# New tables of instruction order for five engines in a hybrid decoder layer on one core

## The chip, the core and the metric

The kernel runs as one program on one core of a Trainium2 chip. The core has five engines with instruction streams of their own: TensorE (PE in the rows; its weight loads are listed apart as PEld), VectorE (DVE), ScalarE (ACT), GpSimd (POOL) and SyncE (SP, which issues the transfers). An engine takes its instructions strictly in the order in which they stand in its stream, and an instruction waits there until what it depends on in other streams is done. The metric is the time of one execution on the device, in microseconds (us); less is better.

## What is computed

One layer of a decoder for a prompt of 512 tokens and 8 sample sequences of one token each, with a width of 1024. The two share all weights, so each matmul runs over 512 + 8 columns, in two halves of 256 and 264. Cut to what matters here:

```python
h = x @ w_in                                       # one input projection for both head groups
# sparse attention: scores with slopes, softmax; compressed, selected and window branch, gated
o_nsa = gates[..., 0:1] * o_cmp + gates[..., 1:2] * o_slc + gates[..., 2:3] * o_win
# gated DeltaNet: convolution, silu, l2norm, then chunks of 64 tokens
qkv, new_gbuf = causal_dwconv(h[..., C_GQKV:C_GA], gdn_buf, gdn_conv_w)
gc = jnp.cumsum(g, axis=-1)
A = jnp.einsum('nbhid,nbhjd->nbhij', kb, k) * dec_strict + jnp.eye(C, dtype=jnp.float32)
X = lax.linalg.triangular_solve(A, rhs, left_side=True, lower=True)
...
vn = val_c - jnp.einsum('bhcd,bhde->bhce', kcd_c, S)
S = S * jnp.exp(gl)[..., None, None] + jnp.einsum('bhcd,bhce->bhde', kend_c, vn)
...
x = layer_norm(DN_ALPHA * x + mix @ w_out, ln_g[0], ln_b[0])
up = x @ ffn_w_up
hg, new_fbuf = causal_dwconv(up[..., :D_FF], ffn_buf, ffn_conv_w)
ffn = (jax.nn.gelu(hg, approximate=False) * up[..., D_FF:]) @ ffn_w_down
x = layer_norm(DN_ALPHA * x + ffn, ln_g[1], ln_b[1])
ple = jax.nn.sigmoid(x @ ple_w_gate) * (p.astype(x.dtype) @ ple_w_proj)
x = layer_norm(DN_ALPHA * x + ple, ln_g[2], ln_b[2])
```

## The kernel before

**Matmuls.** Every weight tile comes from memory as float32 (`raw`, two buffers). ScalarE rounds it to a short form `wh` (L249), and VectorE, or GpSimd for some tiles, subtracts to get the remainder `wl` (L250). `product` then sums three products into a PSUM bank `mm`: `wh` with the high part of the activations (L411), `wl` with the high part (L412), `wh` with the low part (L415). A tile of the input projection with 8 blocks of 128 rows so takes 24 matmuls for each half. Activations carry the same split: `xh`, `xl` for the input, `x1h`, `x1l` behind a norm, `mh`, `ml` for the mixed heads.

**Stages in the profile.** From 0 to about 250 us run the input projection and, woven into it, the convolution of the DeltaNet (L519, L520), its l2norm (L541, L549), the gates and cumulative sums (`g` L588, `gc` L591 and L595), the decay matrices (`exps` L623, `E` L627), `kk` (L634) with the masked products `Lc` and `Lb` (L640, L643), the triangular solve by recursion (`X`, L653 to L682), and the scan over chunks (`vn` L805, `Sd` L810, `S` L814, `Sst` L816, `o` L838, normed at L842 and L845 and transposed to `oT` at L848). The decode step of the samples' DeltaNet state runs beside it: products `stmp` (L862 to L868), the reduction L869, and `so` (L874), a small matmul that needs a PSUM bank of the tag `pg`, of which there are two; VectorE's `inn` (L790) reads `qk` from such a bank. To about 410 us follow attention and output projection: the split keys `KHL` (cast on GpSimd L972, remainder on VectorE L974) and queries `Qs` (L987), scores `S` (L1001), maxima and scaling (`mn` L1008, `rs` L1012 and L1013, `P` L1018 on GpSimd), the copies `qbd` (L1125), the compressed branch `cs` (L1087 to L1099). Then the norm (`acc` L1264, mean `mu` L1274, `R` L1278, L1295 and L1300, splits L1297 to L1302), the FFN's up and down projections to about 780 us, and the layer embedding with the last norms.

**What sets the order.** The code is written in the order of several lists, but what counts is `in_order`. Behind the whole program it takes, for each engine, the instructions as written and chains them anew in the sequence that the table `RUNS` gives: a string of steps, in which `+24` means 24 places on, `-3` back, and `*7` a step repeated. So `RUNS` alone decides which instruction of an engine stands behind which; what is computed, on which engine, and in which buffers does not depend on it. Where several tiles share a tag, the same function also fixes the order of their first uses.

Of the kernel before, what the change touches and what calls it, by code (L numbers as in the profile page):

```python
# [36 lines left out]
def _constants():  # L37
# [70 lines left out]
    SP='+3 -4*3 +2 -2 +1 +3 +1 -6*2 +11 +40 +3 -57 +3 -3 +3 +51 -52 -3 +4 -3 +3 +41 -46 +6 -4 +3*3 +91*2 -93*3 -8 -2 +88 +1 -2 -82 +82*3 +1 -2 -86*2 +2 +2*3 -7 -2 +7 -6*2 +28 -9 +3 +1 -5 +6 +1 +9 -38 +7 +3*2 -5 +4 -5 +4 -5 -11*5 +1 -2 +32 +1 -16 +17 -17 +16 -8 +10 -2 -20*4 +1 -2 +1*2 +14 -12 +11 -11*2 +10 -2 +1 -6 -5*2 +9 +1 +2 +3 +12 -24 +85*2 -86 +1 +32 -33 +1 +43 +1 -43 -4*2 +12 +1*10 +21 -22*3 +20*2 -21*13 +9 -9 +1 +6 -6 +6 -5 +5*2 -5 +4*3 -6 +7*3 -5*2 +3*2 +1 +1*4 -7 +1 +4*2 +2*8 +3 -2 +1*6 -9 -2 +9*5 +2*4 -6*2 +4*15 +2*5 -7*2 +5*5 +2*3 -5*2 +3*13 +11*3 -12*3 -5*2 +3*6 +3 +2*3 -5*2 +3*17 +2*2 -4 +5 -6 +5*3 -6*2',  # L108
)

def in_order(tc, nc):

    of = dict(PE=mybir.EngineType.PE, ACT=mybir.EngineType.Activation, DVE=mybir.EngineType.DVE,
              POOL=mybir.EngineType.Pool, SP=mybir.EngineType.SP)
# [26 lines left out]
def body(tc, nc, ctx, I, O, dbg=None):  # L141
    V, S, G, PE = nc.vector, nc.scalar, nc.gpsimd, nc.tensor
    if dbg is None:
# [1544 lines left out]
```

## Time and profile before

| | us |
|---|---|
| median of 3 runs | 888.88 |
| the three runs | 888.88, 886.75, 889.32 |
| the profiled execution | 887.08 |
| its span in the trace | 885.1 |

The span is what the trace covers from the first to the last instruction; 2.0 us of the profiled execution lie outside it. The clock that was granted to TensorE is 0.995 of full speed over that execution. In the rows below, "busy" is the time in which an engine has an instruction running; several alike are drawn together as "x4" with one duration for all. Waits are put down to the event that ended them.

### The profile page before, as it was taken

Reading aid. Unit: us, or ns where it says so; the run is one execution under the profiler, and the core shown is the slowest. Engines: PE = TensorE matmul, PEld = TensorE weight load, DVE = VectorE, ACT = ScalarE, POOL = GpSimd, SP = SyncE. Lnnn points to the kernel's source line nnn. Section 1 sums busy time; section 2 is a strip of 40 time slices with the busy share of each in tenths; the row PEclk is TensorE's granted clock in tenths of the full one; section 3 lists DMA queues with packets and bytes.
Section 4 is the critical chain, followed back from the end, with each engine's and each line's share of the span. In section 5 each row is a group of like instructions: output and inputs, shape, how many; then the busy total and the mean of one; then the engine's idle time right before and its main releaser. Section 6 shows DMA issues by size and latency. Waiting matters only on the chain.

```text
span 885.1 us, 19223 instructions
## 1 busy us (share of the span) xinstructions
PE 850.9 (96%) x7661; PEld 793.1 (90%) x7661; DVE 585.3 (66%) x1312; ACT 426.8 (48%) x940; POOL 198.4 (22%) x303
## 2 busy tenths in 40 slices
PE   7999999998999999999999999999999999999996
PEld 5988998997888667978899999999999999999985
DVE  3578996678779877788854553344563255577977
ACT  4554538433357886665543432244442144435745
POOL 1133031454413533306710000000000000005332
PEclk9999999999999999999999999999999999999999
DMA  7321323323226240244423243233344133243302
GB/s 210 88 71 50 97 75 100 88 77 81 76 77 209 60 152 18 85 122 120 128 63 118 83 122 96 76 108 104 97 120 121 48 96 90 85 139 119 120 1 97
DMA packets 139112, 85.98 MB, mean 97 GB/s; under 512 B 8318, under 2 KB 130656, under 8 KB 138880
## 3 DMA queue, kind: packets, MB, share of 16 engines
q1 hardware_dynamic: 139024, 84.77, 33.0%
q8 instruction: 60, 0.98, 0.5%
q14 instruction: 28, 0.23, 0.1%
HBM read 79.54 MB, written 7.36 MB: 98 GB/s over the span
## 4 chain that ended last, share of the span: by engine, by line
PE 70%; DVE 16%; ACT 5%; DMA 4%; issue 3%; POOL 1%; SPq 1%; DVEq 0%; ACTq 0%
PE mm L411 18%; PE mm L415 18%; PE mm L412 18%; DVE wl L250 2%; DMA raw<-in_w_out_dram 2%; DVE R L1295 1%; PE PT L1037 1%; DVE qkv L519 1%; DVE X L655 1%; PE S L1001 1%; PE var L1286 1%; DMA raw<-in_w_in_dram 1%; PE pgate L1615 1%; PE pgate L1617 1%; DVE KHL L974 1%
## 5 line engine op out<-in xcount | busy, mean ns | idle before, releaser
L249 ACT CAST wh<-raw 128x512 fp32r<-128x512 f32 x198 | 119.5, 609 | 212.1 <-PE mm L415 189.5
L250 DVE TENSOR_TENSOR wl<-raw,wh 128x512 fp32r<-128x512 f32 (+1 forms) x190 | 131.5, 699 | 125.2 <-ACT wh L249 123.9
L411 PE MATMUL mm<-x1h,wh 128*128 128x256 f32 (+1 forms) x704 | 195.7, 285 | 0.6 <-ACT fcb L1419 0.6
L412 PE MATMUL mm<-x1h,wl 128*128 128x264 f32 (+1 forms) x704 | 195.7, 283 | 0.2 <-POOL wl L250 0.2
L415 PE MATMUL mm<-x1l,wh 128*128 128x264 f32 (+1 forms) x704 | 195.6, 283 | 0.0
L411 PEld LDWEIGHTS mm<-x1h,wh 128*128 128x128 f32 x704 | 131.1, 188 | 1.6 <-ACT fcb L1419 0.8
L412 PEld LDWEIGHTS mm<-x1h,wl 128*128 128x128 f32 x704 | 131.7, 188 | 0.5 <-POOL wl L250 0.4
L415 PEld LDWEIGHTS mm<-x1l,wh 128*128 128x128 f32 x704 | 131.5, 188 | 0.0
L411 PE MATMUL mm<-xh,wh 128*128 128x256 f32 (+1 forms) x408 | 118.7, 298 | 0.3 <-DVE mT L483 0.2
L412 PE MATMUL mm<-xh,wl 128*128 128x264 f32 (+1 forms) x408 | 115.2, 286 | 0.0
L415 PE MATMUL mm<-xl,wh 128*128 128x264 f32 (+1 forms) x408 | 114.3, 286 | 0.0
L412 PE MATMUL mm<-hhl,wl 128*128 128x256 f32 (+1 forms) x352 | 97.9, 283 | 0.0
L411 PE MATMUL mm<-hhl,wh 128*128 128x264 f32 (+1 forms) x352 | 97.0, 284 | 0.3 <-DVE R L1507 0.3
L415 PE MATMUL mm<-hhl,wh 128*128 128x256 f32 (+1 forms) x352 | 96.7, 283 | 0.0
L411 PEld LDWEIGHTS mm<-xh,wh 128*128 128x128 f32 x408 | 76.8, 190 | 4.5 <-ACT z L203 0.7
L1431 POOL COPY last<-fcb 128x10 f32<-128x10 f32 x22 | 8.9, 405 | 310.5 <-ACT fcb L1419 294.7
L412 PEld LDWEIGHTS mm<-xh,wl 128*128 128x128 f32 x408 | 77.1, 190 | 0.8 <-issue 0.5
L415 PEld LDWEIGHTS mm<-xl,wh 128*128 128x128 f32 x408 | 76.9, 190 | 0.4 <-issue 0.2
L412 PEld LDWEIGHTS mm<-hhl,wl 128*128 128x128 f32 x352 | 65.7, 188 | 0.1
L411 PEld LDWEIGHTS mm<-hhl,wh 128*128 128x128 f32 x352 | 65.3, 188 | 0.5 <-DVE R L1507 0.5
L415 PEld LDWEIGHTS mm<-hhl,wh 128*128 128x128 f32 x352 | 65.2, 188 | 0.1
L1300 POOL TENSOR_SCALAR R<-R,vec 128x264 f32<-128x264 f32 (+1 forms) x40 | 28.7, 730 | 67.9 <-ACT x1h L1297 50.3
(453 smaller groups left out, 1868.8 us busy)
## 6 DMA issues: line engine op xcount, KB each, us to landing
raw<-in_ffn_w_up_dram SPq DMA_DIRECT2D x44, 512.0 KB
raw<-in_w_in_dram SPq DMA_DIRECT2D x25, 512.0 KB
raw<-in_w_out_dram SPq DMA_DIRECT2D x32, 256.0 KB
raw<-in_ffn_w_down_dram SPq DMA_DIRECT2D x16, 512.0 KB
pg<-in_cache_nsa_kv_dram SPq DMA_DIRECT2D x16, 256.0 KB
praw<-in_ple_w_gate_dram SPq DMA_DIRECT2D x8, 512.0 KB
raw<-in_ffn_w_down_dram SPq DMA_DIRECT2D x8, 384.0 KB
xr<-in_x_prompt_dram SPq DMA_DIRECT2D x16, 128.0 KB
```

Of the source, the lines that this page charges most:

```text
L249: both = (S.copy(th[:, :k1 - k0, :M], raw[:, k0:k1, :M]), low.tensor_tensor(tl[:, :k1 - k0, :M], raw[:, k0:k1, :M], th[:, :k1 - k0, :M], o ...
L250: low.tensor_tensor(tl[:, :k1 - k0, :M], raw[:, k0:k1, :M], th[:, :k1 - k0, :M], op=ALU.subtract))
L411: PE.matmul(o, hs[k], rh[hv][k], start=(k == ks[0]), stop=False)
L412: PE.matmul(o, ls[k], rh[hv][k], start=False, stop=False)
L415: PE.matmul(o, hs[k], rl[hv][k], start=False, stop=(k == ks[-1]))
L519: V.scalar_tensor_tensor(y[:, :T], cb[:, k:k + T], gcw[:, k, j:j + 1], y[:, :T], op0=ALU.mult, op1=ALU.add)
L655: V.tensor_tensor(X[:, j + 1:32, 0:j + 1], X[:, j + 1:32, 0:j + 1], tv, op=ALU.add)
L974: V.tensor_tensor(kl[d2 * 64:d2 * 64 + 64, :T], kvf[f][r0, :T], kh[r0, :T], op=ALU.subtract)
L1001: PE.matmul(ps[:, :wm], q_[:, ts_], kh[:, :wm], start=True, stop=False)
L1037: PE.transpose(pt[:, g4 * 128:g4 * 128 + 128], P[g4][:, st * 128:st * 128 + 128], ident)
L1300: G.tensor_scalar(r, r, b_, 1.0, op0=ALU.add, op1=ALU.mult)
L1431: G.tensor_copy(rows[:, :, f % 4], cb[:, 512:522])
```

## The change

Only the five strings of `RUNS` differ, one for each engine. A line of it:

```diff
-    POOL='+63 -64 +61 +40 +14 -118 +1 -2 +1*2 +1 +1 -4 +1 +1*6 +18 -19 +2*2 +14*2 +1 -22 +51 -48 ...
+    POOL='+63 -64 +61 +40 +14 -118 +1 -2 +1*2 +1 +1 -4 +1 +1*6 +18*3 +1 -23 +2*2 -4 +4*2 -6 +18 ...
```

Every engine has exactly the instructions that it had, with the same operands: 6759 on TensorE, 1314 on VectorE, 867 on ScalarE, 308 on GpSimd, 359 on SyncE. 3372 of TensorE's stand at another place, 630 of VectorE's, 308 of ScalarE's and 105 of GpSimd's; most by a few places.

The first place is TensorE's stream behind the convolution's tile `mm_1135`, where `l2s` and `l` are the l2norm's sums and `gc` the first cumulative sums; `mm_1184` and `mm_1210` are the next tile of the input projection. Rows with a minus stood there before, rows with a plus stand there now:

```order
 L412 MATMUL mm_1135<-xh_15_86,wl_1106 128x264
 L415 MATMUL mm_1135<-xl_16_87,wh_1105 128x264
-L541 MATMUL l2s_640<-sq_632,cst 128x8
-L541 MATMUL l2s_640<-sq_634,cst 128x8
+L541 MATMUL l2s_640<-sq_636,cst 128x8
 L549 MATMUL l_84_648<-sq_632,cst 128x512
-L549 MATMUL l_85_654<-sq_634,cst 128x512
-L591 MATMUL gc_613<-g,cst 128x32 x2
-L549 MATMUL l_86_660<-sq_636,cst 128x512
 L411 MATMUL mm_1184<-xh_1_72,wh_1176 128x256
 L411 MATMUL mm_1210<-xh_1_72,wh_1176 128x264
```

`gc` and two of the `l` leave this place. The first `gc` now stands 33 matmuls later, with `exps` behind it, and the second 73 matmuls later, behind the tile `mm_1258`.

The second place is TensorE's stream between the two halves `mm_2834` and `mm_2860` of one tile:

```order
 L412 MATMUL mm_2834<-xh_15_86,wl_2831 128x256
 L415 MATMUL mm_2834<-xl_16_87,wh_2830 128x256
-L874 MATMUL so_2922<-sgd_2004,cst 64x64 x3
 L411 MATMUL mm_2860<-xh_1_72,wh_2826 128x264
 L412 MATMUL mm_2860<-xh_1_72,wl_2827 128x264
```

The `so` that stood between the two halves is gone from there, and the 24 matmuls of `mm_2860` follow at once. At their end the stream reads:

```order
 L415 MATMUL mm_2860<-xl_16_87,wh_2830 128x264
-L848 MATMUL oT_3004<-cst,o_2958 128x128 x4
+L848 MATMUL oT_3004<-cst,o_2958 128x128
+L874 MATMUL so_2922<-sgd_2004,cst 64x64 x3
 L751 MATMUL ktm_3013<-cst,qkv_295 128x128
+L848 MATMUL oT_3004<-cst,o_2958 128x128
 L751 MATMUL ktm_3013<-cst,qkv_370 128x128
+L919 MATMUL kvT_2888<-cst,kvf_339_2823 128x128 x2
 L751 MATMUL ktm_3013<-cst,qkv_444 128x128
+L848 MATMUL oT_3004<-cst,o_2958 128x128 x2
```

Three of the four matmuls of `so` now stand behind `mm_2860` and behind one transpose `oT`, which needs `o` from VectorE.

The third place is VectorE's stream in the attention. `qbd` are copies of 64x8 elements that set up the samples' queries; `rs_3918` are the factors of four heads, on which GpSimd's scaling `P_3933` waits. Before:

```order
L1087 TENSOR_TENSOR cs_3843<-cs_3838,cb_3844 128x512
L1125 COPY qbd_3989<-qks 64x8 x5
L1008 ISA P_4199,mn_4183<-S_4196,dist_3278 128x256
L1008 ISA mn_4183 128x1
L1012 RECIPROCAL rs_3918<-rs_3918 128x4
L1125 COPY qbd_3989<-qks 64x8
L1008 ISA P_4188,mn_4183<-S_4191,dist_3278 128x256
L1008 ISA mn_4183 128x1
L1013 TENSOR_TENSOR rs_3918<-rs_3918,sig 128x4
L1090 TENSOR_REDUCE cmn_3847<-cs_3843 128x32
L1125 COPY qbd_3989<-qks 64x8 x2
L1008 ISA P_4199,mn_4183<-S_4202,dist_3278 128x256
```

And now:

```order
L1125 COPY qbd_3989<-qks 64x8 x6
L1012 RECIPROCAL rs_3918<-rs_3918 128x4
L1125 COPY qbd_3989<-qks 64x8 x2
L1013 TENSOR_TENSOR rs_3918<-rs_3918,sig 128x4
L1008 ISA P_4199,mn_4183<-S_4196,dist_3278 128x256
L1008 ISA mn_4183 128x1
L1087 TENSOR_TENSOR cs_3843<-cs_3838,cb_3844 128x512
L1008 ISA P_4188,mn_4183<-S_4191,dist_3278 128x256
L1008 ISA mn_4183 128x1
L1090 TENSOR_REDUCE cmn_3847<-cs_3843 128x32
```

All eight copies stand ahead of the finished `rs_3918` (L1013), and `cs` and its reduction behind it. On GpSimd, the stream changes at the norm at 430 us, too: the first scaling L1300 of `R_517` stands one place earlier, ahead of the `wl` with which it stood in turn, and a second one comes before the last of the four `wl`.

## Rows read from the trace of the kernel before

**Rows 1.** The page: span, busy time by engine, chain by engine, one group
```profile
span 885.1 us, 19223 instructions
...
PE 850.9 (96%) x7661; PEld 793.1 (90%) x7661; DVE 585.3 (66%) x1312; ACT 426.8 (48%) x940; POOL 198.4 (22%) x303
...
PE 70%; DVE 16%; ACT 5%; DMA 4%; issue 3%; POOL 1%; SPq 1%; DVEq 0%; ACTq 0%
...
L1300 POOL TENSOR_SCALAR R<-R,vec 128x264 f32<-128x264 f32 (+1 forms) x40 | 28.7, 730 | 67.9 <-ACT x1h L1297 50.3
```

**Rows 2.** Busy us (x instructions) of PE, PEld, DVE, ACT, POOL in two stages
```profile
100.00:150.00 50.00, 48.96 (x558) 45.31 (x558) 43.12 (x94) 30.35 (x58) 11.86 (x16) 1.00 0.32 85
...
450.00:500.00 50.00, 50.00 (x412) 49.44 (x411) 23.70 (x48) 18.40 (x35) 1.96 (x9) 1.00 0.31 96
```

**Rows 3.** Waits of TensorE by releaser: us in total, times, longest us
```profile
PE so L874 <- DVE inn L790: 2.7, 1, 2.7
PE S L1001 <- DVE mn L1008: 2.2, 3, 1.1
...
PE mu L1274 <- DVE acc L1264: 1.4, 1, 1.4
...
PE gc L591 <- DVE g L588: 1.1, 1, 1.1
...
PE X L682 <- ACT Ys L676: 0.8, 1, 0.8
...
PE soT L886 <- DVE inn L790: 0.7, 1, 0.7
```

**Rows 4.** Duration ns min/median/max of four lines' instructions on VectorE
```profile
L1295 DVE SCALAR_TENSOR_TENSOR R<-R,vec,rstd x40: 473/486/1521, 401.1 to 872.9; 128x264 f32<-128x264 f32 x24, 128x256 f32<-128x256 f32 x16
...
L1278 DVE TENSOR_TENSOR R<-R,mu x40: 410/422/429, 391.8 to 858.8; 128x264 f32<-128x264 f32 x24, 128x256 f32<-128x256 f32 x16
...
L250 DVE TENSOR_TENSOR wl<-raw,wh x190: 404/690/1756, 19.5 to 790.6; 128x512 fp32r<-128x512 f32 x182, 128x256 fp32r<-128x256 f32 x8
...
L987 DVE SCALAR_TENSOR_TENSOR Qs<-qf,Qs x8: 685/1006/1395, 222.7 to 267.8; 64x512 fp32r<-64x512 f32 x8
```

**Rows 5.** Timeline (start us, us), 200 to 206 us, VectorE, then GpSimd
```profile
200.18 2.35 DVE L250 TENSOR_TENSOR wl<-raw,wh 128x512 fp32r<-128x512 f32 x2
...
203.47 2.71 DVE L974 TENSOR_TENSOR KHL<-kvf,KHL 64x512 fp32r<-64x512 f32 x3
...
200.15 1.83 POOL L931 TENSOR_TENSOR VV<-kvo,VV 128x512 fp32r<-128x512 f32 x1
201.94 3.70 POOL L972 CAST KHL<-kvf 64x512 fp32r<-64x512 f32 x4
```

**Rows 6.** Timeline, 222 to 227 us, VectorE, then GpSimd
```profile
222.67 4.07 DVE L987 SCALAR_TENSOR_TENSOR Qs<-qf,Qs 64x512 fp32r<-64x512 f32 x4 [0.26 <-ACT Qs L986]
...
222.52 3.67 POOL L972 CAST KHL<-kvf 64x512 fp32r<-64x512 f32 x4
```

**Rows 7.** Timeline, 278 to 283 us, VectorE, then GpSimd
```profile
278.00 0.78 DVE L1125 COPY qbd<-qks 64x8 f32<-64x8 f32 x5
...
280.69 1.61 DVE L1125 COPY qbd<-qks 64x8 f32<-64x8 f32 x2
...
280.21 1.04 POOL L1018 TENSOR_TENSOR P<-P,rs 128x512 f32<-128x512 f32 x1 [8.18 <-DVE rs L1013]
```

**Rows 8.** Timeline, 418 to 434 us, VectorE and GpSimd in turn
```profile
419.28 2.64 DVE L1264 TENSOR_TENSOR acc<-acc,R 128x264 f32<-128x264 f32 x2
...
418.92 4.13 POOL L250 TENSOR_TENSOR wl<-raw,wh 128x512 fp32r<-128x512 f32 x3 [0.65 <-ACT wh L249]
...
430.47 3.17 DVE L1295 SCALAR_TENSOR_TENSOR R<-R,vec,rstd 128x264 f32<-128x264 f32 x3 [2.39 <-ACT rstd L203]
...
430.19 2.75 POOL L250 TENSOR_TENSOR wl<-raw,wh 128x512 fp32r<-128x512 f32 x2 [3.16 <-ACT wh L249]
```

More of the change, by code (lines that the diff above doesn't have):

```diff
@@ new lines @@
+    ACT='+26 -27*10 +17 -18*16 +5*2 -5*2 +7*2 -6 -4 +12*2 -11*2 +3 +9*2 -15 +14 -12 +11 -12 +3 -4 +51*2 -50*2 +5 +46*2 -48 -7 +6*2 +3 -4*2 +47 -48 +47 -12*2 -33 +32 -37 +3 +35 +9 -40 +39 -6 -48 +41*2 -38*2 +49*2 -11 -41 +40 -40 -9 +6 -7 +7 +42 -42*2 +44 -45 +16 +11 -7 +24 -14 +13 -5 +8 -5 +4 -18 +1 +5 +13*2 -11*2 -12 +14 -10 +18*2 -11 -5 +4 +3 +7*2 -9 -5 +4 +9 -7 -4 +6 +2 -7 +6 +1*2 -3 +15 -14 +13 +10 -25 +24 -34 +8 +4 -5 +1 +2 -5 +1 +8 -7*2 -87*3 +3 +100 -103 +1 +79 -89 +8 -11 +4*2 +4*2 -14 +90 -78*2 +90 +4 -17 +22*2 -13 -12*2 +10*2 -12 +13 -14 +24*2 -13 -14*3 +12 -2 -12 +12*2 +2 +12*2 -14*2 +3 +21*2 -23 +1*4 -10 +4 +12 -7 +6*2 +12*2 -22*5 +9 +1*4 +9*2 -16 +9 +1*2 -21 +17 -18 +12 -13 +22 +4 -16 -13 +12 +6 +7 -6 +11 +12 -28 +2*3 +2 +24 +4 -30 +6 -7*4 +3*3 +3*3 +26 -38 +13 -4 +3*2 -12 +11 +15 -28*2 +32 -28 +42 -38 +5*2 -7 +6*2 +5 -6*2 +1 +6 -5 -5 -8 +58 -48 +5 +15 -15 -2 +49 -56 +32 -51 +55 -33 +27 -2 -27 +31 -20*2 +13 -34 +37 +5 -39 +32 -59 +101 -39 -39 +32*2 -33 +38 +5 -47 +40*2 -41 +40 -6*2 +7 -45*2 +43*2 +2 -48 +47 -3 -2 +5 -51 +50*2 -5*2 +5 -3*2 +3*2 +2 -3*2 -56 +91 -97 +53*2 -50 -2 +55 -54 +53 -56 +55*2 -56 +59 -5 +4 -5 +4 -62*2 +60*4 +2 -67 +64 -2 +2*2 -63*2 +61 -69 +68*3 +5 -6 +5*3 +6 -74 +66*2 +1*3 +5*2 -5 -66 +48*4 +13 +3*3 -42 +42*2 +5 -6 +5 -6 +5 -20 +13*2 +8 -5*2 -6 +5 -20 +19 +1*2 +15*2 -17 -19 +18 +33 -34 +33 -34*2 +33 -22 -13*2 +11 +21 -22*2 -14*2 +12 +19 -33 +12 -13 +12*2 +17 -18 -15*4 +11*3 +14*2 -16 +9 -3 -7 +13 -16 +2*2 +30 -34 +33*5 -25*8 +17*2 -19 +22 -23 +8 -9 +16 +4 -5 -18 +17 -18*2 +16 -17*2 +17 -18*2 +20 +7*2 -14*2 +3*2 -5 +5*2 +6 -3 -5 +4 +5 -5 +4 -20 +3 +10 +4 -5 +4 +5*2 -7 +6 -7*3 +4 +5*3 -7 -2 +7 -7 -26 +8 +8 +7 +5 -6 +9*2 -6*2 +4*2 -6 +5 -6 +9*2 -6*2 +4*2 -6*2 +4*13 +4*2 -6*2 +4*2 -6*2 +4 +4*2 -6*2 +4*2 -6*2 +4 +4*2 -6*2 +4*2 -6*2 +4 +4*2 -6*2 +4*2 -6*2 +4 +4*2 -6*2 +4*2 -6*2 +4 +4*2 -6*2 +4*2 -6*2 +4 +4*2 -6*2 +4*2 -6*2 +4 +4*2 -6*2 +4*2 -6*2 +4*13 +4*2 -6*2 +4*2 -6*2 +4 +4*2 -6*2 +4*2 -6*2 +4 +4*2 -6*2 +4*2 -6*2 +4 +8*2 -10*2 +8*2 -10*2 +8 -9 +12 -13 +7 +4 -5 +4 -14 +13 -14 +7*2 +4 +5*2 -7*2 +5*2 -7 +1 -2 +5*12 +18*2 -20*8 +12 -13*2 +3 -2 -3 +4 -2 +7 -7 +6 -3 -11 +5 +15 -10*2 +8 -9*4 +5*2 +2*8 -17*3 +4*2 +8*2 +8 +2 -3 -10 +1 -2 +12 -3 +2 -3 +2 -7 -8*3 +13*3 -16*2 +14*3 -8*2 +6 +5 -6 +5 -6 +5*6 -11*3 +11*2 +2*2 -9 +4 -5 +4 +2*5 +1 -2 +1*2 -16 +19 -5*2 +3 -4*2',
@@ new lines @@
+    POOL='+63 -64 +61 +40 +14 -118 +1 -2 +1*2 +1 +1 -4 +1 +1*6 +18*3 +1 -23 +2*2 -4 +4*2 -6 +18 +31 -31*2 +1 +1 +1 -6 -17*2 -6 +2 +2*3 +13 +1 +1*5 +2 -3*2 +2*2 -3 -26*4 +24*4 +2 +3 -4 +12 +3 -17*2 +15 -14 +1 -2 +2 +1 +3 -6 +35 -39 +5 +8 +1*2 -3 -9 +30 +1 -38 +8 +26 -19*4 -15 +2 -3 +6*2 +22 -23 +20 -17*4 +4*2 +8 -8 -2 -6 +16*2 +1 -2 -19*2 +12*2 +17 -12*2 -3 -2 +11 +1*2 +3 -2 -3*2 +3 +1 -2 -3 -17 +1 +19 -2 -18 +1 +13 +2 -19 +1 -7 +1 +21 +1 -4 +1 +1 +2 -3*2 +4 -4*3 +2*2 -3 +2 +3 -4 +1 -2 +2 +1 -2 +2 -2 +1 +2*2 -4 +5 +1 -2 +1 -6 -4 +3 +19*4 -19*4 +8*3 +4 -16 +15*2 -17 +16 -17*6 +11*2 +1 -2 +1*6 +1 -2 +1*30 +2 +1 -2 +2 +3 -11 +6 -3 -5 +7 +1 -4 +3*6 +1 -2 +1*3 +1 -2 +1*12 +6 -6 +3 +1 -4 -5 +2 -2',
@@ new lines @@
+    SP='+1 +1 -4 +1 +2 -2 +1 +3 +1 -6*2 +9 +1 +42 -55 +3 +53 -49 -9 +3*2 -3 +2 +47 -5 -37 -5*2 +3*3 +91*2 -93*3 -8 -2 +88*5 -85 +84 +1 -2 -86*2 +2 +2*3 -7 -2 +7 -5 -2 +29 -9 +3 -3 +3 +2 +1 +9 -38 +7 +3*2 -5*3 +2*2 -15*7 +31 +1 -16 +17 -17 +16 +3 -12 +9 -20*4 +18 -18 -2 +1*2 +3 +11 -11*2 +10*2 -3 -4 -5*2 +9 +1 +2 +3 +12 -24 +85*2 -86 +1 +32 -33 +1 +43 +1 -43 -4*2 +12 +1*10 +21 -22*3 +20*2 -21*13 +9 -9 +1 +6 -6 +6 -5 +5*2 -5 +4*3 -6 +7*3 -5*2 +3*2 +1 +1*4 -7 +1 +4*2 +2*8 +3 -2 +1*6 -9 -2 +9*5 +2*4 -6*2 +4*15 +2*5 -7*2 +5*5 +2*3 -5*2 +3*13 +11*3 -12*3 -5*2 +3*6 +3 +2*3 -5*2 +3*17 +2*2 -4*2 +4*4 -6*2',
```

7 lines of the change are left out of this document (2 added, 5 removed).

## Prediction

> **What bounds the kernel now.** I read the page first. TensorE is busy 850.9 of a span of 885.1 us, and the chain that ended last is 70% TensorE, 16% VectorE [rows 1]. So at most 885.1 - 850.9 = 34.2 us are TensorE's to win back, and a new order wins only where TensorE stands still and VectorE is what it waits for. The table by stage says where that is not: from 450 to 500 us TensorE is busy all 50.00 us, 412 matmuls at 50.00 / 412 = 0.121 us each [rows 2]. It looks so up to about 750 us, while GpSimd does next to nothing there (1.96 us of the same 50). A third of the run can neither gain nor lose from keeping GpSimd and VectorE apart.
>
> The waits of TensorE by releaser come next. The reader is to see that few waits are long and that the releaser is nearly always VectorE: `so` 2.7 us in one piece, `S` 2.2 in three, `mu` 1.4, `gc` 1.1, `X` 0.8 (behind ScalarE, which VectorE's recursion feeds), `soT` 0.7: 8.9 us together [rows 3].
>
> Then the same VectorE instruction at different times. L1295, two inputs in SBUF, takes 486 ns at the median and up to 1521; L250 690 and up to 1756; L987 685 at the least and 1006 at the median; L1278, of the first one's shapes but with one input in PSUM, takes 410 to 429 ns in all 40 cases [rows 4]. What lies beside the long ones is GpSimd arithmetic on SBUF. In the stretch at 200 us a pair of `wl` takes 2.35 us where two medians are 1.38, while GpSimd runs `VV`; three `KHL` take 2.71 instead of 3 x 0.685 = 2.06, beside GpSimd's four casts [rows 5]. At 222 us four `Qs` take 4.07 instead of 2.74 beside four more casts [rows 6]. At 280.7 us two tiny `qbd` copies take 1.61 us where five of them had taken 0.78, that is 0.16 each; GpSimd multiplies `P` from 280.21 on [rows 7]. At 419 us two `acc` take 2.64 instead of about 2 x 0.43 beside `wl` on GpSimd, and at 430 us three `R` take 3.17 instead of 3 x 0.49 [rows 8]. The lengthening in these six pieces is 1.0 + 0.65 + 1.3 + 1.3 + 1.8 + 1.7 = 7.8 us; they are about half of what I count along the chain.
>
> **The change, place by place.** No instruction is added, removed or altered; the same 9,600 or so stand in another order on their engines. So the cost is only in who waits for whom. I go through TensorE's waits and read from the two orders what now stands before each.
>
> `gc` at 55 us. Before, TensorE takes `gc` right behind the convolution's statistics and stands 1.1 us for `g` [rows 3]. Now the matmuls of the next input tiles come first, some 33 ahead of the first `gc` (33 x 0.121 = 4.0 us of cover). The wait goes: -1.1 us (between 0, if it returns at a later reader of the same chain, and -1.1).
>
> `so` at 208 us. It waits 2.7 us, not for its own operand but for the bank that VectorE's `inn` reads last (L790). Now 24 matmuls stand in front of it, 24 x 0.121 = 2.9 us, so with VectorE unchanged the wait is gone. VectorE does change: the reduction and the scaling of `o` (about 0.69 each, the 512-wide price of rows 4) and the other `inn` (0.42, as L1278) now come before the last `inn`, +1.8 us; the `wl` pair has moved ahead of the stretch, which saves its lengthening of 1.0 and up to 1.4 of its own time if it fills a gap there. Net +0.8 to -0.6, which leaves a wait of 2.7 + 0.8 - 2.9 = 0.6 at the worst; if something else collides with `VV` in its place (1.0), 1.6. Gain 1.1 to 2.7; I take 2.0. GpSimd's casts and VectorE's `KHL` keep their order, so that lengthening stays.
>
> `soT` and `Qs` at 222 to 234 us. GpSimd's casts and VectorE's `Qs` and `KHL` stand as before, so their lengthening stays too. Only TensorE's own order helps: `soT` goes behind a tile of 24 matmuls, which covers its 0.7. I take -0.6 (0 to -1.2, the latter if the wait behind it goes as well).
>
> `S` at 281 us. Before, GpSimd's `P_3933` was free to run as soon as `rs_3918` was there, and two `qbd` copies stood behind `rs_3918` on VectorE. Now all eight copies stand ahead of `rs_3918`, so `P_3933` cannot run beside them: this collision is removed by data dependence, not by timing. TensorE's longest wait there is about half of 2.2; I take -1.1 (0 to -2.2). `cs` moves behind, and the next `rs` still lies near GpSimd's `cs`.
>
> `mu` at 421 us. The last `acc` of VectorE and the `wl` subtractions of GpSimd keep their order, so the 1.8 us of lengthening there stays. TensorE has about six more matmuls in front of `mu`: 6 x 0.121 = 0.7 of the 1.4. I take -0.7 (0 to -1.4).
>
> The norm at 430 to 440 us. GpSimd's first `R_517` comes ahead of a `wl`, which opens a gap beside VectorE's `R`: one of the lengthenings of about 1.0 us goes, and about half of it is TensorE's. -0.5 (0 to -1.0).
>
> The end. The same kind of step (L1300, 0.73 us each [rows 1]) for the second quarter of the features now comes last on GpSimd, a pair is 1.5 us. Most of it lies beside TensorE's last tiles: +0.5 (0 to +1.5).
>
> Sum: -1.1 - 2.0 - 0.6 - 1.1 - 0.7 - 0.5 + 0.5 = -5.5 us. With every term at its best the sum is -9.6, at its worst -1.1 + 1.5 = +0.4. The profiled execution took 887.1 us, 2.0 of it outside the span, and is 1.8 below the median of the three runs, 888.9. 887.1 - 5.5 = 881.6, and on the scale of the median 883.4; I say 883.
>
> The Trainium skill, page "SBUF — State Buffer", section "Who interferes with whom", says that a VectorE instruction with two SBUF inputs and a GpSimd instruction that reads SBUF share one port pair, held by one of them for a whole instruction while the other blocks completely. The lengths in rows 4 to 8 agree in kind. By that rule port time is only handed over, not lost, so that two streams kept apart need as long as two streams that collide, and the contention part of the change would be worth nothing; that is the first rival.
>
> **The rivals.** First: the waiting only moves. At `acc`, `L1295` or `Qs` GpSimd has its own queue to get through, and what it does not do beside one VectorE instruction it does beside the next; `Qs`, `KHL` and the `acc` do not even change places. Then only TensorE's own cover is left, and part of it comes back as other waits: `gc` 1.1 and about half of `so`, 1.3, less 0.5 at the end is -1.9, which gives 887.0. Against it: at `qbd` the collision is excluded by a dependence, and GpSimd is busy only 22% of the span [rows 1], so it has idle time to move into.
>
> Second, slower: the delta rule's chain starts later. Half of `gc` (and what its cumulative sums feed: the decay matrices, `kk`, the recursion on VectorE, then `X` on TensorE) now stands behind some 73 matmuls, 73 x 0.121 = 8.8 us. For it: TensorE already waits 0.8 us at `X` [rows 3], so the chain has no slack at its end, and VectorE is busy 43.12 of 50 us from 100 to 150 [rows 2], so it cannot catch up much. Against it: TensorE's first decay matmuls (`exps`) come earlier than before, and the last ones about 30 places later, which is 30 x 0.121 = 3.6 us. If the whole 8.8 us reached `X`, the sum is -5.5 + 8.8 = +3.3: 892.2. It decides the sign from a delay of 5.5 us on.
>
> Third: nearly full separation. If the lengthening along the chain goes wherever it is, twice the 7.8 us of rows 5 to 8, some 15 us at most; with the parts that the order visibly leaves I say -13, which gives 876. For it: many small moves on VectorE and GpSimd that I did not price one by one. Against it: the three stretches named above that keep their order.
>
> **How the numbers follow.** Forecast of 883 (its own range 879 to 886, from the bounds -9.6 to about -2.5): 0.50. Waiting moves, 887: 0.18. Slower, 892: 0.17. Full separation, 876: 0.15. A change under 0.3%, 2.7 us, cannot be told from none, so faster is below 886.2 and slower above 891.6. Faster takes the forecast, the third rival and a little of the first, less an edge: 0.65. Slower, with an end that is later than I think: 0.17. Same: 0.18. The range from 874 to 891 takes in the third rival and the first, and leaves out the upper half of the second and the far end below.
>
> **What would show it.** Right: TensorE's wait at `so` at 208 us under 1 us with 24 matmuls of the same weights ahead of it; `gc` without a wait; all `qbd` copies at 0.16 to 0.17 us and no wait of TensorE at `S` near 281; L1295's maximum well under 1.5 us; `Qs`, `KHL` and `acc` as long as before. A span about 5 us shorter by 450 us, and the stretch from 450 to 750 unchanged. Wrong: a wait at `kk` or `X` of several us between 75 and 150; a lead at 450 us that is lost behind 800; or VectorE's lengthening the same in sum with other instructions bearing it. What would upset the whole reading is a gain in the stretch where TensorE is full, since nothing here speaks for one.

## The result and the profile after

The changed kernel took 878.78 us (median of 4 runs, 877.23 to 879.31) where the kernel before took 888.04 beside it: a ratio of 0.9893, 95% interval 0.9871 to 0.9914. Timed once more on the chip of the experiments it took 879.05 against 885.5, a ratio of 0.9916 (0.9893 to 0.9939), which is -7.4 us (the ratio on record is not the quotient of the two medians, which are 6.45 us apart; all differences below are worked out from such ratios). The forecast was 883, that is -5.5 from the profile, faster with a chance of 0.65.

The page of the changed kernel, its span, its busy times and its chain by engine, answers to [rows 1]:

```profile
span 877.3 us, 19202 instructions
...
PE 851.4 (97%) x7661; PEld 791.9 (90%) x7661; DVE 577.6 (66%) x1312; ACT 428.3 (49%) x940; POOL 194.1 (22%) x303
...
PE 80%; DVE 9%; ACT 4%; DMA 4%; issue 2%; SPq 1%; POOL 0%; DVEq 0%; POOLq 0%; ACTq 0%
```

VectorE's busy time is 7.7 us less with the same instructions, so some of the lengthening is gone; whether that is what shortens the kernel is another question, which two of the experiments answer. Its share of the chain is 9% where it was 16%, and TensorE's 80% where it was 70%. The waits of TensorE (us in total, times, longest), against [rows 3]:

```profile
PE X L682 <- ACT Ys L676: 1.4, 2, 1.0
...
PE mm L411 <- ACT wh L249: 0.9, 1, 0.9
...
PE S L1001 <- DVE mn L1008: 0.9, 2, 0.5
...
PE mu L1274 <- DVE acc L1264: 0.9, 1, 0.9
...
PE mm L411 <- ACT R L1349: 0.3, 1, 0.3
...
PE so L874 <- DVE sgd L869: 0.3, 1, 0.3
...
PE kk L634 <- DVE Lb L643: 0.2, 1, 0.2
```

`so` is down from 2.7 to 0.3 us, `S` from 2.2 to 0.9, `gc` and `soT` are gone from the list; `X` has grown from 0.8 to 1.4, and a wait of 0.9 for a weight (`wh`) is new. Two of these lines answer waits of before that are not among [rows 3]:

```profile
PE mm L411 <- ACT R L1349: 2.2, 2, 1.9
...
PE kk L634 <- DVE Lb L643: 1.5, 2, 1.3
```

The durations (ns, min/median/max) of VectorE's instructions, against [rows 4] and, for `qbd`, [rows 7]:

```profile
L1295 DVE SCALAR_TENSOR_TENSOR R<-R,vec,rstd x40: 471/489/1542, 394.8 to 866.5; 128x264 f32<-128x264 f32 x24, 128x256 f32<-128x256 f32 x16
...
L250 DVE TENSOR_TENSOR wl<-raw,wh x190: 402/692/1553, 18.0 to 785.0; 128x512 fp32r<-128x512 f32 x182, 128x256 fp32r<-128x256 f32 x8
...
L987 DVE SCALAR_TENSOR_TENSOR Qs<-qf,Qs x8: 686/1036/1530, 218.8 to 262.5; 64x512 fp32r<-64x512 f32 x8
...
L1125 DVE COPY qbd<-qks x8: 159/170/172, 271.7 to 273.1; 64x8 f32<-64x8 f32 x8
```

Here the reader is to see what did not happen: L1295 still reaches 1542 ns, `wl` 1553, `Qs` has a higher median than before. Only the `qbd` copies are clean, none above 172 ns. The separation is partial, and most of the gain must be looked for elsewhere.

Where it came, by the same event in both traces. `mu`, the first matmul of the norm, starts at 414.64 us and started at 421.97, so 7.3 of the 7.8 us between the spans are won by then. From 450 to 750 us TensorE is full in both, as forecast. The first steps of the lead lie at the start, of which the prediction says nothing. TensorE's timeline after (start us, us) begins:

```profile
5.92 1.04 PE L347 MATMUL xT<-cst,xr 128*128 128x128 f32 x8
...
7.73 1.09 PE L347 MATMUL xT<-cst,xr 128*128 128x128 f32 x8 [0.77 <-DMA xr<-in_x_prompt_dram]
```

Before, the first `xT` ran at 7.29 and the second eight at 9.38 (`xr` had not landed); now they run at 5.92 and 7.73. SyncE's new table issues the first piece of `x` ahead of the first weights (at 0.75 us, before at 1.80). Then at `so`, TensorE's timeline:

```profile
203.45 0.39 PE L411 MATMUL mm<-xh,wh 128*128 128x264 f32 x1 [0.46 <-ACT kvf L913]
...
206.94 0.33 PE L848 MATMUL oT<-cst,o 128*128 128x128 f32 x1 [0.30 <-DVE o L845]
...
207.27 0.56 PE L874 MATMUL so<-sgd,cst 128*64 128x64 f32 x6
```

and VectorE's:

```profile
200.27 0.67 DVE L838 TENSOR_TENSOR o<-o,o 128x512 f32<-128x512 f32 x1
...
201.89 2.74 DVE L974 TENSOR_TENSOR KHL<-kvf,KHL 64x512 fp32r<-64x512 f32 x3
...
206.80 0.74 DVE L790 TENSOR_TENSOR inn<-qk,inn 128x256 f32<-128x256 f32 x2
```

TensorE goes from one half of the tile to the other with a wait of 0.46 us, then waits 0.30 at `oT`, and `so` follows at once. VectorE has done `o` (L838) ahead of the `KHL`, which take 2.74 us, as long as before [rows 5]. Then a place where time was lost, `X`:

```profile
146.61 0.24 PE L682 MATMUL X<-Ys,TN 32*32 32x32 f32 x2 [0.99 <-ACT Ys L676]
...
148.34 0.90 PE L751 MATMUL ktm<-cst,qkv 128*128 128x128 f32 x3
```

And the stages by window (length, then busy us of PE, PEld, DVE, ACT, POOL; the granted clock is the third number from the end):

```profile
145.00:155.00 10.00, 8.65 (x112) 8.23 (x111) 3.81 (x8) 6.03 (x12) 0.20 (x1) 0.83 0.40 108
...
205.00:215.00 10.00, 9.39 (x87) 8.33 (x86) 9.38 (x22) 4.86 (x15) 3.77 (x5) 1.00 0.18 54
...
415.00:420.00 5.00, 5.00 (x27) 4.34 (x27) 3.07 (x9) 3.61 (x10) 4.71 (x6) 0.70 0.70 205
```

In the ten microseconds around `X` the granted clock is 0.83: for a part of them TensorE ran at the lower of its two levels, 1.2 GHz instead of 2.4. In this execution it also fell at 415 us, behind the two waits at `wh` and `mu`:

```profile
413.39 0.39 PE L411 MATMUL mm<-x1h,wh 128*128 128x256 f32 x1 [0.93 <-ACT wh L249]
...
414.64 1.25 PE L1274 MATMUL mu<-acc,cst 128*128 128x264 f32 x2 [0.86 <-DVE acc L1264]
```

In a second execution (`after_again` below) it did not fall there: the same window has 1.00.

### The profile page after: what moved, and what is told of

It reads as the page before. It is cut to its first block, busy times and chain, and to the rows that moved or that the text cites. A ratio compares the mean times of both kernels' runs of the same rounds, so it can differ in the third digit from the quotient of the medians.

```text
span 877.3 us, 19202 instructions
## 1 busy us (share of the span) xinstructions
PE 851.4 (97%) x7661; PEld 791.9 (90%) x7661; DVE 577.6 (66%) x1312; ACT 428.3 (49%) x940; POOL 194.1 (22%) x303
## 4 chain that ended last, share of the span: by engine, by line
PE 80%; DVE 9%; ACT 4%; DMA 4%; issue 2%; SPq 1%; POOL 0%; DVEq 0%; POOLq 0%; ACTq 0%
PE mm L411 20%; PE mm L415 20%; PE mm L412 20%; PE PT L1037 1%; DVE wl L250 1%; PE mm L1580 1%; PE mm L1581 1%; PE mm L1582 1%; PE var L1286 1%; PE pgate L1615 1%; DMA xr<-in_x_prompt_dram 1%; DMA raw<-in_w_out_dram 1%; PE pgate L1617 1%; PE pgate L1616 1%; ACT wh L249 1%
## 5 line engine op out<-in xcount | busy, mean ns | idle before, releaser
L412 PE MATMUL mm<-x1h,wl 128*128 128x256 f32 (+1 forms) x704 | 196.4, 284 | 0.0
L412 PE MATMUL mm<-hhl,wl 128*128 128x264 f32 (+1 forms) x352 | 98.3, 283 | 0.8 <-DVE wl L250 0.8
L1300 POOL TENSOR_SCALAR R<-R,vec 128x264 f32<-128x264 f32 (+1 forms) x40 | 27.3, 693 | 71.6 <-ACT x1h L1297 51.0
```

What stands on the lines that cost most here:

```text
L412: PE.matmul(o, ls[k], rh[hv][k], start=False, stop=False)
L1300: G.tensor_scalar(r, r, b_, 1.0, op0=ALU.add, op1=ALU.mult)
```

## The experiments

Tables can be spliced in time: the instructions that ran in a stretch of the old trace take the new order there, all others keep the old one, on all five engines. (In the strings, `-29*7` is one step of -29 and then seven instructions in a row; the step itself is not repeated.) Most kernels below are such splices, or take a single table; a line of an edited table is shown for each, cut. All times are against the kernel before, run beside them on the same chip (two chips were used, with 885.5 and 885.6 us).

**SyncE's table alone.**

```diff
-    SP='+3 -4*3 +2 -2 +1 +3 +1 -6*2 ...
+    SP='+1 +1 -4 +1 +2 -2 +1 +3 ...
```

> The kernel before with the new table for SyncE alone: 42 of its 309 positions differ, no other engine's order changes. Theory (start): the new order issues the first piece of x ahead of the first weights and the old conv rows earlier, TensorE's first transposes start about 1.7 us sooner and its 1.5 us wait at gstT shrinks to about 0.6; with the clock kept up behind it the gain is 2 to 3.4 us, about 885.5. Rival (chance): the 3.4 us that separate the two traces by 30 us are how transfers happened to land in those two executions, and this table is worth nothing: 888, within 0.3 per cent.

885.96 us, ratio 0.9998 (0.9982 to 1.0014). No gain in the time. In its trace the first `mm` of the input projection is early, at 17.0 us against 18.2 to 18.9 in the eight traces with the old order at the start, but at 24.4 us TensorE then waits 0.95 us for ScalarE (`cb`). At its 241st matmul it stands at 39.4 us, no earlier than two of those eight (39.3), so the lead is lost by then. Its clock also fell behind the old wait at `so`, which in the profiled execution before it had not; but it falls there in most executions with the old order (last section). The same window of both, before first:

```profile
205.00:215.00 10.00, 7.25 (x71) 6.45 (x70) 8.89 (x16) 3.50 (x8) 3.89 (x6) 1.00 0.22 64
```

```profile
205.00:215.00 10.00, 8.86 (x71) 8.25 (x72) 7.41 (x16) 3.40 (x10) 1.86 (x5) 0.83 0.18 52
```

**From 30 to 155 us.**

```diff
-    DVE='... -125 +8 -9*2 +128*2 -123 -8*4 +4*2 +3 -4*2 +124*2 ...
+    DVE='... -125 +8 -9*4 +126 -122 +121 -128*2 +4*2 +3 -4*2 ...
```

> The new order on all engines only for the instructions that ran from 30 to 155 us before, the old order elsewhere. My prediction: gc's wait of 1.1 us goes, -1.1 us, 887. Rival (the delta chain is late): the chain behind gc reaches X later, TensorE waits there, and its clock halves for a few us behind the wait, as the trace after shows at 146 to 152 us: nothing gained or up to +2 us, 888 to 890; equal work stood at +3.4 us ahead at 30 us and +2.4 at 160, so +1.0.

888.95 us, ratio 1.0028 (1.0011 to 1.0045): 2.5 us slower. The wait at `gc` is gone, and that at `kk` is down to 0.2, but `X` waits as in the changed kernel:

```profile
PE X L682 <- ACT Ys L676: 1.4, 2, 1.0
```

and its clock over 145 to 155 us is 0.83 too. The second rival's mechanism is there, with a small wait and a spell of half clock instead of 8.8 us. VectorE's busy time, on the other hand, is 3.6 us less than before, in a kernel that is slower:

```profile
PE 854.0 (96%) x7661; PEld 795.8 (90%) x7661; DVE 581.7 (66%) x1312; ACT 426.5 (48%) x940; POOL 197.5 (22%) x303
```

**From 155 to 250 us.**

```diff
-    POOL='... -14 +1 +13 -16 +8 -7 +1 -2 -3 +5 ...
+    POOL='... -14 +1 -2 +2 +1 +3 -6 +35 -39 +5 ...
```

> The new order only for what ran from 155 to 250 us. My prediction: so -2.0 and soT -0.6, together -2.6 (bounds -1.1 to -3.9), 885.4; casts and KHL still collide. Rival (waiting moves): the wait at so comes back at oT or at the next user of the banks, -1 or less, 887. The two traces part by 2.1 us between 160 and 250 us.

882.48 us, ratio 0.9959 (0.9938 to 0.9980): -3.6 us, the largest part. The wait at `so` is down to 0.3 us, with 0.5 for `kvf` ahead of it, and the clock stays at 1.00 over 205 to 215 us. VectorE's busy time is 1.2 us more than before:

```profile
PE 848.6 (96%) x7661; PEld 790.8 (90%) x7661; DVE 586.5 (67%) x1312; ACT 426.8 (48%) x940; POOL 197.2 (22%) x303
```

So the stretch that gains most does so with VectorE no less busy, and the one that is slower has it less busy: the shorter busy time of VectorE is not what the time follows.

**From 250 to 450 us.**

```diff
-    POOL='... -23 +20 -17*2 +1 -2 +5*2 +8 -8 -7 +4 ...
+    POOL='... -23 +20 -17*4 +4*2 +8 -8 -2 -6 +16*2 +1 ...
```

> The new order only for what ran from 250 to 450 us. My prediction: S at 281 -1.1, mu -0.7, the norm -0.5, together -2.3 (0 to -4.6), 885.7. Rival (separation): with qbd, R, acc and x1l all kept clear of GpSimd the lengthening on the chain falls by some 6 us here and TensorE gains 4 or more, 884 or less. Rival (waiting moves): 0 to -1. The two traces part by 2.7 us between 250 and 450 us.

886.73 us, ratio 1.0004 (0.9984 to 1.0024): nothing that the time can tell, and not the 4 us or more of separation. Its waits at `S` are 0.9 us as in the changed kernel. In the trace the stretch itself is shorter, but some 2 us are lost again behind it (table further down).

**The whole again, without a part, the last part, the first part.**

```diff
-    PE='... -3 +2 -29*7 +22 -23*6 +17*2 -19*9 +10*2 -12 +11*3 ...
+    PE='... -3 +2 -29*24 +5*22 +2*4 -6*2 +4*18 +2 -3*2 +1*12 ...
```

is the line of `r1_start` and of `not_r2`; of `r5_450_end` it is

```diff
-    POOL='... -2 -6 +17*10 +1 -2 +1*30 +2 +1 -5 +2 ...
+    POOL='... -2 -6 +17*2 +1 -2 +1*6 +1 -2 +1*30 +2 ...
```

> The changed kernel once more, beside the parts and on their chip. Four parts measured alone gave 0, +2.5, -3.6 and +0.4 us, together about -0.7, where the whole was 9.3 us faster. If the parts add up, with little to come from the start's other engines and from the last stage, the whole comes out near -1 to -3 on this chip; if it is again near -9, the parts hang together: a part alone leaves waits, and spells of half clock behind them, that the whole avoids.

> The new order everywhere but for the instructions that ran from 30 to 155 us before, which keep the old one. Delta-chain theory: the new order there costs 2.5 us (late X, then half clock), so this version is 2 to 3 us faster than the changed kernel. Rival (the part is late only because the parts around it kept the old order): not faster than the changed kernel, or slower by up to 2.

> The new order only for what ran after 450 us. My prediction: nothing from 450 to 750, and +0.5 at the end (0 to +1.5). From the two traces: equal work stands 7.2 us ahead at 450 us and the spans differ by 7.8, so -0.6. Theories of separation give a gain at 800 to 880 us of up to 1.5, where R L1295 and x1l are lengthened.

> The new order on all engines only for the first 30 us. Theory (start): TensorE's transposes begin earlier, the wait at gstT is shorter and no spell of half clock follows it at 19 to 23 us: -1 to -3.4 us. SyncE's table alone gave 0.0 with 1.4 us either way although its trace was 1.2 us ahead of the other old-start runs at 20 us; the same is expected here, -1 to -1.5, more if ScalarE's and VectorE's few moves there count.

`after_again` 879.05, ratio 0.9916 (0.9893 to 0.9939). `not_r2` 879.68, 0.9920 (0.9896 to 0.9944): no faster than the changed kernel, so the part that costs 2.5 us alone costs nothing that the time can tell in the whole (the trace can, see the table). `r5_450_end` 885.68, 0.9993 (0.9976 to 1.0009): -0.6, no loss at the end that the time shows. `r1_start` 884.24, 0.9980 (0.9957 to 1.0003): -1.8, just short of clear.

**One move on TensorE.** Of the kernel before, `so` alone:

```diff
 L415 MATMUL mm_2834<-xl_16_87,wh_2830 128x256
-L874 MATMUL so_2922<-sgd_2004,cst 64x64 x3
 L411 MATMUL mm_2860<-xh_1_72,wh_2826 128x264
...
 L415 MATMUL mm_2860<-xl_16_87,wh_2830 128x264
+L874 MATMUL so_2922<-sgd_2004,cst 64x64 x3
 L848 MATMUL oT_3004<-cst,o_2958 128x128 x4
```

> The kernel before with one move on TensorE alone: the first three matmuls of so stand behind the 24 matmuls of mm_2860 instead of ahead of them. VectorE's and GpSimd's orders are the old ones, so every collision of theirs stays. Cover theory: the wait at so (2.7 us) is gone or under 0.3, and with it the spells of half clock at 205 to 212 us that five of six runs with the old order there showed: -2.7, up to -4 us where a spell goes too, about 882. Separation theory (the gain of that stretch came from VectorE's wl, KHL and o being clear of GpSimd): under -1, 885.

885.36 us, ratio 0.9988 (0.9973 to 1.0003). Neither theory had the cause. The waits:

```profile
PE S L1001 <- DVE mn L1008: 2.6, 4, 1.1
...
PE mm L411 <- ACT kvf L913: 2.4, 1, 2.4
```

The wait is not gone; it has another name. TensorE's timeline, and ScalarE's below it:

```profile
207.14 0.59 PE L411 MATMUL mm<-xh,wh 128*128 128x264 f32 x1 [2.38 <-ACT kvf L913]
...
207.97 0.42 PE L411 MATMUL mm<-xh,wh 128*128 128x264 f32 x1
...
210.95 0.28 PE L411 MATMUL mm<-xh,wh 128*128 128x264 f32 x1
```

```profile
206.20 0.63 ACT L840 ACTIVATE osq<-o 128x512 f32<-128x512 f32 x1 [5.73 <-DVE o L838]
...
206.74 0.35 ACT L913 COPY kvf<-mm 128x256 f32<-128x256 f32 x1
```

The second half of the tile needs a PSUM bank that ScalarE empties with `kvf` (L913), and `kvf` stands on ScalarE behind `osq` (L840), which waits for VectorE's `o` (L838), which stands behind three `KHL`. Two waits lay side by side there and ended within a microsecond of each other; the trace before shows the one that TensorE met first. The spacing of 0.66 us for three matmuls at 207.97 and of 0.36 at 210.95 is half and full clock: the granted clock is 0.50 from 208 to 210 us and 1.00 from 211.

**The same move undone in the changed kernel.** The diff is the one above with its signs turned, but that one `oT` stands ahead of the removed row.

> The changed kernel with that one move undone: so's first three matmuls again ahead of mm_2860, all other orders new. Cover theory: the wait comes back, as long as VectorE's inn is late (two more instructions stand ahead of it now), 2.7 to 3.5 us, with half clock behind it in most runs: +2.7 to +5, 882 to 884. Separation theory: with VectorE's stretch cleared the wait is short, under 1.5 us, and the time rises by less than 1.5.

886.02 us, ratio to the kernel before 0.9999 (0.9983 to 1.0016). The changed kernel's ratio is 0.9916, so this is some 7 us above it, more than expected. TensorE's timeline:

```profile
209.18 0.90 PE L874 MATMUL so<-sgd,cst 128*64 128x64 f32 x6 [4.25 <-DVE inn L790]
...
210.84 0.42 PE L411 MATMUL mm<-xh,wh 128*128 128x264 f32 x1
```

4.25 us of wait, since VectorE's `inn` now has the reduction L842 and the scaling L845 ahead of it, and half clock behind it (three matmuls in 0.66 us). With three small matmuls in the old place no gain is left. The wait of 4.25 less the 0.76 (0.46 + 0.30) that the changed kernel waits there, and a spell of half clock of 1.7 (last section), account for some 5 of the 7 us at the place. In this profiled execution another 2 us were lost in the first 40, with a wait of 1.8 us at `xT` and a spell of half clock at 18 us, which this move does not touch.

**One move on VectorE.** Of the kernel before, `qbd` alone:

```diff
+L1125 COPY qbd_3989<-qks 64x8 x2
 L1013 TENSOR_TENSOR rs_3918<-rs_3918,sig 128x4
 L1090 TENSOR_REDUCE cmn_3847<-cs_3843 128x32
-L1125 COPY qbd_3989<-qks 64x8 x2
```

> The kernel before with one move on VectorE alone: the last two qbd copies stand ahead of rs_3918, so that GpSimd's P_3933, which waits for it, cannot run beside them. My prediction: the copies take 0.17 us each instead of 0.59 and 1.01, and TensorE's wait at S of 1.1 us behind them goes: -1.1 us, 884.4, which the time alone can just not tell from none. Rival (waiting moves): P_3933 lies beside another two-operand instruction of VectorE that becomes as long, and S waits as before: 0.

885.21 us, ratio 1.0001 (0.9983 to 1.0018); the time cannot tell it. The trace can. The durations of the eight copies, in this kernel and in `so_move`, which has the old order there:

```profile
L1125 DVE COPY qbd<-qks x8: 157/170/173, 278.1 to 280.3; 64x8 f32<-64x8 f32 x8
```

```profile
L1125 DVE COPY qbd<-qks x8: 157/170/1007, 277.8 to 281.1; 64x8 f32<-64x8 f32 x8
```

and TensorE's waits at `S`:

```profile
PE S L1001 <- DVE mn L1008: 2.1, 5, 0.7
```

No copy is lengthened. The wait of TensorE behind them is gone; first the kernel before, then this one:

```profile
282.82 0.38 PE L1001 MATMUL S<-KHL,Qs 128*128 128x256 f32 x1 [1.14 <-DVE mn L1008]
```

```profile
281.67 0.38 PE L1001 MATMUL S<-KHL,Qs 128*128 128x256 f32 x1
```

`P_3933` now lies beside a reduction, which takes 0.68 us as before. But a part of the collision has moved on. GpSimd's next `P`, 0.6 us later than it was, meets an `ml` of 128x8 elements that took 0.14 us before:

```profile
282.84 1.04 POOL L1018 TENSOR_TENSOR P<-P,rs 128x512 f32<-128x512 f32 x1
```

```profile
282.90 1.00 DVE L1314 TENSOR_TENSOR ml<-mixs,mh 128x8 fp32r<-128x8 f32 x1
```

and TensorE waits 0.44 us at a later `S`. Of the 1.1 us some 0.8 are left: from its 2901st to its 3120th matmul TensorE takes 29.5 us here and 30.3 in `so_move`, and in total it waits 2.1 us at `S` where the kernel before waits 2.2 and `so_move` 2.6.

**Two parts together.** From 155 to 450 us, the tables of `r3_155_250` and `r4_250_450`.

> The new order for what ran from 155 to 450 us, the two stretches that gave -3.6 and +0.4 alone. If they add up: -3.2, 882.3. If stretches hang together (a stretch with the old order before it runs into half clock or late operands that it does not cause): -5 to -6, 880.

883.53 us, ratio 0.9972 (0.9956 to 0.9988): -2.5. They add up within their intervals; nothing is gained by the two together.

## Why the prediction was right in direction and size, point by point

The direction and the size came out, the sum behind them only in part. By stretches (start, 30 to 155, to 250, to 450 us, end) the forecast was 0, -1.1, -2.6, -2.3 and +0.5; taken alone they measured -1.8, +2.5, -3.6, +0.4 and -0.6. That -5.5 stands beside -7.4 is partly luck: a gain that had no term offsets a loss whose term had the wrong sign.

**The waits that were left out.** "Few waits are long" and "the releaser is nearly always VectorE" were read from a list without `R` 2.2 (behind ScalarE), `xT` 1.7 and `gstT` 1.5 (behind transfers) and `kk` 1.5 us, 6.9 us beside the 8.9 that are in it. In the trace of the changed kernel these four are 2.1 us.

**The start, missed.** For the same reason "I go through TensorE's waits" had no term for the first 30 us. The stretch gave -1.8 us (-3.8 to +0.3, `r1_start`), just short of clear, about as much as the largest term of my sum. SyncE's table is not enough for it: alone its lead is lost by the 241st matmul, while with the other engines' new order TensorE is there 1.5 us earlier (37.8 in `r1_start`, 39.4 in `e_sp`).

**`so`.** The forecast took 2.0 us from 24 matmuls of cover, and 0.6 for `soT` in the same stretch, which gave 3.6 (1.8 to 5.5). That the cover is needed is shown by `after_so_back`; that it is not enough is shown by `so_move`, whose 1.1 us are not clear of nothing and whose trace has 0.1 us (table below). The step that failed is "with VectorE unchanged the wait is gone": VectorE unchanged, `kvf` holds the next bank for 2.4 us. What the new order does about it, by the trace, is `o` five places earlier on VectorE, ahead of `KHL`; no run makes that move alone. I had read it only as work that comes before the last `inn`. It is a matter of dependences; the lengthening of `KHL` stayed.

**`gc`.** Its wait went, as said, and the stretch still cost 2.5 us (1.0 to 4.0) alone. The term -1.1 has the wrong sign by itself; what stands in its place is the second rival's mechanism at a fraction of its price. The wait at `kk` went too, 2.4 us with `gc`, but by the 1273rd matmul, where `X` begins, TensorE has gained only 0.5 to 1.0 us in the four profiled executions with this order. From there to the 1601st they take 17.8 to 18.0 us and the ten others 16.1: 0.6 us more of waiting at `X` and a spell of half clock, which all four have there and none of the ten. The stretch so costs 0.9 to 1.4 us in the traces, in the changed kernel as well as alone.

**`S` at 281 us.** Right in kind: the copies are clean and the wait is down from 2.2 to 0.9, though not gone. One dependence by itself is worth 0.8 us there (`qbd_move`); the whole new order takes 2.0 us off the same matmuls (28.3 for 30.3 us), by what else was not tried. This is the one place where keeping the engines apart is shown to shorten TensorE's way, and even there GpSimd met another instruction instead.

**`mu` and the norm.** `mu` waits 0.86 instead of 1.44, as the six matmuls of cover say, but 0.93 us at a weight stands ahead of it, and in two of the six profiled executions with this order half clock behind it. The waits of the norm's stretch (0.19 and 0.59 before) are gone although `R` and `x1l` are lengthened as before, up to 1542 ns. "L1295's maximum well under 1.5 us" was wrong. A wait that I had not priced, 1.9 us at 409 us for the residual `R` (L1349), is gone from the place, 0.3 us are left.

**The end.** The time, -0.6 (-2.1 to +0.8), does not decide between +0.5 and a small gain.

**The rivals.** "The waiting moves" is true of `so_move` to the letter and of `qbd_move` in part, of the kernel as a whole not. Full separation did not come: the three stretches said to keep their order kept their lengths within half a microsecond (eight `Qs` 7.7 and 7.9 us, eight `KHL` 7.1 and 6.7, the last six `acc` before `mu` 5.6 and 6.0). The Trainium skill, page "SBUF — State Buffer", section "Who interferes with whom", says that the shared port pair is held for a whole instruction and the other engine blocks completely. At `qbd` the traces agree: the copies of 0.16 us and the `ml` of 0.14 took up to 1.0 us beside a `P` of 1.04, while `P` itself took no longer for it. So the time lost depends on what GpSimd's instruction meets, which the first rival's "only handed over" did not say. The same section says that reductions never contend on this chip, and the one beside `P_3933` takes 0.68 us, as does the reduction L915 of an input of the same size, 128x512, at 213 us, where GpSimd is idle.

**What stays open.** The five stretches alone sum to -1.8 + 2.5 - 3.6 + 0.4 - 0.6 = -3.1 us, the whole is -7.4. Adding the half-widths of the five intervals as squares gives 3.9, with the whole's 2.0 about 4.4, so the gap of 4.3 is at the edge of what the times leave. The traces leave less. Up to its 241st, 1601st, 2773rd and 4182nd matmul, TensorE has done the same matmuls (by line, operands and shape) in all 14 profiled executions, in whatever order; the time between these points (us, range, number of executions) is:

| matmuls | in the trace before | old order there | new order there |
|---|---|---|---|
| to the 241st | 0 to 41 us | 39.3 to 41.2 (8) | 37.8 to 39.8 (5) |
| to the 1601st | to 161 | 119.4 to 119.7 (10) | 120.6 to 120.7 (4) |
| to the 2773rd | to 247 | 86.4 to 90.7 (7) | 84.1 to 85.0 (5) |
| to the 4182nd | to 443 | 193.7 to 195.3 (7) | 190.6 to 193.7 (6) |
| to the end | to 885 | 442.3 to 442.5 (7) | 441.7 to 442.5 (5) |

Not in the table, since they have neither order whole: `e_sp` at the start, 39.4; to the 2773rd matmul `after_so_back`, 90.0, and `so_move`, 87.7 (`qbd_move`, with the old order there and as much half clock, has 87.8); `qbd_move` to the 4182nd, 193.0; and at the end `r4_250_450` and `r34`, 444.8 and 444.1. These two, with the old order behind the new one, lose some 2 us there that the whole does not, about what they gained to the 4182nd; what they lose it to was not tried. The spread within a field is mostly half clock: from the 1601st to the 2773rd matmul the old order has up to 10.2 us of it in one execution, the new order none, and where the fields of the next row touch, the executions with the new order include two with 3.4 us of it.

The changed kernel gains 3.4 - 1.0 + 2.3 + 2.5 + 0.5 = 7.7 us on the kernel before, of 7.8 between the spans. So the stretches to 250 and 450 us gain about what was forecast (2.6 and 2.3), and the start makes up for what `X` costs (more than that in this pair, since the kernel before also had half clock at 19 us).

## What to carry to other kernels

When a wait is to be covered by moving other work ahead of it, look for the second wait beside it: ask what the work that is moved up needs (its bank, who empties that, what that engine stands behind), because the trace names only the wait that was met first. Read the transfer engine's stream of an order table as closely as the others. And count what contention costs only where the lengthened instruction is the last one that a reader waits for. Remove it by a dependence rather than by timing, which shifts with every other change, and ask what the other engine's instruction meets in its place. When a time cannot tell what a part is worth, compare the traces between points up to which the same work has been done.

## What the hardware showed that I had not expected

Waits of TensorE cost more than their length. Over 205 to 215 us the granted clock was 0.66 to 0.83 in eight of the nine profiled executions that have a wait of 2.4 us or more there (`so` at its old place, or `kvf`), the profiled execution of the kernel before being the ninth with 1.00; in all five without such a wait (the changed kernel twice, `not_r2`, `r3_155_250`, `r34`) it was 1.00. The window of 205 to 215 us in `after_so_back` (columns as above):

```profile
205.00:215.00 10.00, 5.61 (x34) 5.26 (x34) 6.10 (x10) 2.08 (x6) 5.22 (x7) 0.83 0.00 0
```

The granted clock is 0.83, and TensorE is busy in 5.61 of the 10 us: the wait took most of the rest. At 0.83 over 10 us, 1.7 us of full speed are lost on top of the wait. The same was seen at `X`: where TensorE waits there 0.99 and then 0.36 us (four executions) the granted clock over 145 to 155 us is 0.83, and where it waits 0.7 to 0.8 once (the ten others) it is 1.00. At `so` the price varies from one execution to the next, and the spread of the kernel before goes with it: in 88 timed runs its median is 888.8 us in the 15 with a mean granted clock up to 0.990 and 883.9 us in the 13 from 0.997 on; a straight line through all 88 gives some 0.65 us for each 0.001. The medians are 0.994 for the kernel before and 0.996 for the changed one, so by estimate about 1.3 of the 7.4 us come by way of the clock, which the forecast had no term for, and 6.1 remain beside its 5.5.
